# Two-layer decoder trunk: first layer up to its norm rewritten, with no large GpSimd operations in that stretch

## Chip, cores, metric

One core of a Trainium2 chip. The metric is the device time of one execution in microseconds (us). The engines are called as the profile calls them: PE (TensorE), DVE (VectorE), ACT (ScalarE), POOL (GpSimd), SP (SyncE, which here only issues DMAs). Each has its own instruction stream, and they meet at semaphores.

## What is computed

Two layers on 512 tokens of width 1024; the feed-forward width is 2816. All is float32. Cut to what matters here:

```python
mod = silu(c) @ ada_w + ada_b            # six vectors of 1024 per layer: t1, s1, g1, t2, s2, g2
h = x * (1 + s1) + t1
a, u, v = split(h @ w_in)                # 4 groups of 128 | 512 | 512
pooled = (cs - prev) / cnt - a           # trailing windows 2, 4, 8, 16 over the tokens
pool = (pooled @ pool_w) * pool_scale
v = layernorm(gelu(v)) * sgu_ln_g + sgu_ln_b
z = tril(sgu_w) @ v + sgu_b              # per head, in chunks of 128 tokens
f = concat(pool, gelu(u) * z) @ w_out
x = layernorm(ALPHA * x + g1 * f)        # n1
...                                      # channel mixing with t2, s2, g2, then n2
```

## The kernel before

Every product is done as three float32r matmuls: a weight is split into a rounded upper part `whi` and the rest `wlo`, an activation into `hh` and `hl`, and `mm3` adds up whi·hh, whi·hl and wlo·hh. A weight of 128x1024 (512 KB) goes through `load` (L65, issued by SP), a cast on ACT to `whi` (L132) and a subtraction to `wlo` (L135), which `refill` puts on DVE or, with `G`, on POOL. Seven raw buffers (`N_RAW`) hold weights and adaLN matrices alike; a load waits until the operation that read its buffer before is done.

The adaLN vectors are sums on DVE (`ada_sum`, L182): a 128x1024 piece of `ada_w` times silu(c), accumulated to one column. Sixteen of them (`raw_first`) give t1 and s1 of the first layer, 24 more (`raw_ada`) the three vectors that its first norm needs. `pump` puts them between other work; each step also issues loads `ADA_AHEAD` steps ahead.

The scheduler is manual: each engine takes its instructions as the code writes them, and SP its DMAs. The stages of the first layer:

1. The first stage, a loop over the eight k-tiles of h: two sums (L182), A0 and B0 (L462, L465), `hh` on DVE (L466), the same in float32 on ACT (L467), `hl` (L468, on DVE for k below 2, else on POOL), and the products of this k-tile for the four tiles of a and the four chunks of v, 192 matmuls of 512 columns in all.
2. Token mixing: copies of a (L532), trailing sums (L540, L541) and pooled (L550 to L553), the norm of v (gelu L574, statistics L577, `rstd_of` L272 to L275 with the power on POOL, two DVE operations L280 and L283), four tiles of u, `pool_mix` (L560 to L565), `z_mms` (L603) and `z_mix` (L586 to L597).
3. The projection with `w_out`, the second half of it in `project_and_norm`: per chunk the residual (L291, L292), statistics (L377), `rstd_of`, the application (L383), the transposition on PE (`turn`, L298) and `modulate` (L310 to L313), which gives the `hh` and `hl` that the next products read. The lower parts of the next weights are made in it, on POOL (`refill(..., G, lows)`).
4. `after_norm`, the next stage's first four tiles; `next_residuals` then runs eight operations on POOL (L318, L319) that multiply the norm's rows g and b (loaded by L325, scaled on ACT, L327) into xr. `project_and_norm` and `next_residuals` run three times: at the norm n1 of layer 0, at n2 of layer 0 and at n1 of layer 1.

Of the kernel before, what the change touches and what calls it, by code (L numbers as in the profile page):

```python
# [8 lines left out]
F32 = mybir.dt.float32  # L9
# [18 lines left out]
N_UNITS, N_RAW, N_SPLIT = 29, 7, 6  # L28
AHEAD, ADA_AHEAD = 2, 3
PRE_FILL, FILL = 6, (0, 2, 2, 2, 2, 3)  # L30
# [8 lines left out]
def trunk(ctx: ExitStack, tc: tile.TileContext, a: dict, out: bass.AP):  # L39
# [5 lines left out]
    wraw = ctx.enter_context(tc.tile_pool(name="wraw", bufs=N_RAW))  # L45
    wsplit = ctx.enter_context(tc.tile_pool(name="wsplit", bufs=N_SPLIT))
# [4 lines left out]
    # each engine takes its instructions in the order they are written here  # L51
# [24 lines left out]
    A.activation(c_th, c_in, AF.Tanh, scale=0.5)  # L76
    V.scalar_tensor_tensor(c_th, c_th, 1.0, c_in, op0=ALU.add, op1=ALU.mult)
    c2 = const.tile([P, D], F32, name="c2")
    for hf in range(2):
        ps = bank(f"c2_{hf}")  # L80
        for j in range(4):
            k = 4 * hf + j
            T.matmul(
                ps[:, j * P : (j + 1) * P], c_th[:, k : k + 1].to_broadcast([P, P]), ident, start=True, stop=True
            )
        A.copy(c2[:, halves(hf)], ps)
    ones = const.tile([P, P], F32, name="ones")
    V.memset(ones, 1.0)
# [4 lines left out]
    rcnt = const.tile([P, 16], F32, name="rcnt")  # L93
    modc = [const.tile([P, 48], F32, name=f"modc{l}") for l in range(L)]

    # ---- the weights in the order of their use: float32 in, two float32r parts out
# [56 lines left out]
    def refill(n=1, eng=None, defer=None, in_units=False):  # L153
        """Prepares the next n weights, as far as there is room for them."""
        for _ in range(n):
            if count["split"] < len(order) and (in_units or count["live"] < N_SPLIT):
                wsplit_next(in_units, eng, defer)
                while count["load"] < min(len(order), count["split"] + count["ahead"]):
                    wload()

    def get():
        assert ready
        return ready.pop(0)
# [4 lines left out]
    def mm3(ps, w, x, start, stop):  # L168
        """ps += (wh + wl).T @ (xh + xl)"""
# [4 lines left out]
    # ---- adaLN: columns of silu(c) @ ada_w, 128 at a step, that fill in between other work  # L174
# [54 lines left out]
    def pump(n=1, upto=None):  # L229
        """n steps of the sums, as far as these are for the vectors upto."""  # L230
# [14 lines left out]
    def weave(gens, side=()):  # L245
        """The steps of gens in turn, those of side in between."""
# [6 lines left out]
    def affine_cols(l, sub, g, b):  # L253
        """Columns A, B with h = n * A + B, from the last norm's g and b and the modulation."""
# [14 lines left out]
    # ---- post-norm: xr holds the sum; leaves n, h, and the next residual  # L269
# [8 lines left out]
    def affine_norm(t, mv, rs, g, b, pieces=1, after=None):  # L278
        """t = (t - mean) * rstd * g + b"""
# [7 lines left out]
    def residual(ps, c, hf, gate, eng=None, f=slice(0, HALF)):  # L287
        """Columns f of half hf."""
# [5 lines left out]
    def turn(c, tag):  # L294
        """n of one chunk, transposed."""
# [5 lines left out]
    def modulate(c, ps, tag, AB):  # L301
        """h of one chunk from its transposed n, in two halves."""
# [27 lines left out]
    def pair_mms(ps, c, w, act, i, n, f=slice(0, HALF)):  # L330
        """A pair of k-tiles i, i + 1 of n, for columns f of one chunk."""
# [8 lines left out]
    def project(act, hf, name, after):  # L340
        """All chunks at once against streamed weights; after(i) follows each pair."""
# [11 lines left out]
    def project_and_norm(act, ps0, gate, tag, AB):  # L353
        """The second half chunk by chunk, each chunk's norm under the next one's products.
        ps0 holds the first half. Leaves the last chunk to be turned."""
# [5 lines left out]
        for c in range(NCH):  # L361
# [6 lines left out]
            if c == NCH - 1:  # L368
                refill(4 - len(ready), G, lows)
# [16 lines left out]
            if c + 1 < NCH:  # L386
                residual(ps0[c + 1], c + 1, 0, gate, G)

    def project_and_end(act, ps0, gate, grow, brow):
        """The same at the end, where the norm goes out; the last chunk's columns in two parts."""  # L390
# [7 lines left out]
        def first_half(c):  # L398
            sts[c] = small.tile([P, 4, 6], F32, tag="st4", name=f"end{c}")
            residual(ps0[c], c, 0, gate, G)  # L400
# [47 lines left out]
    # ---- start: modulation of the first layer and h from x, one k-tile after the other  # L448
# [3 lines left out]
    def first_load(k):  # L452
        x = unit(f"xT{k}")
        raw = [load(a["ada_w"][0, v, k], f"first{v}_{k}") for v in (1, 0)]
# [3 lines left out]
    def first_h(k, x, raw):  # L458
# [21 lines left out]
    tiles, v_w = [], []  # L480
    for k in range(KD):
# [23 lines left out]
    wload(3)  # L505
    refill(1, G)
    count["ahead"] = AHEAD
    done = [ps for ps, w in tiles]

    for l in range(L):  # L510
        col = cols[l]

        # ======== token mixing
# [19 lines left out]
        sums = []  # L533

        def window_sums(g, eng):
            s = at[g]
            for i in range(g + 1):
                d = 1 << i
                n = unit(f"ws{g}_{i}")
                eng.tensor_tensor(n[:, d:], s[:, d:], s[:, : S - d], op=ALU.add)  # L540
                eng.tensor_copy(n[:, :d], s[:, :d])  # L541
                s = n
            sums.append(s)

        pooled = []

        def pool_group(g):
            w, s = WINDOWS[g], sums[g]
            t = unit(f"pooled{g}")
            V.scalar_tensor_tensor(t, s, 1.0 / w, at[g], op0=ALU.mult, op1=ALU.subtract)  # L550
            e = small.tile([P, 16], F32, tag="edge", name=f"edge{g}")
            V.tensor_tensor(e[:, : w - 1], s[:, : w - 1], rcnt[:, : w - 1], op=ALU.mult)
            V.tensor_tensor(t[:, : w - 1], e[:, : w - 1], at[g][:, : w - 1], op=ALU.subtract)  # L553
            pooled.append(t)

        mix = [None] * 8

        def pool_mix(g):
            ps = bank(f"pm{g}")
            T.matmul(ps, poolw[:, g * P : (g + 1) * P], pooled[g], start=True, stop=True)  # L560
            sc = col[:, C_PS + g : C_PS + g + 1]
# [22 lines left out]
        def z_mix(h):  # L584
            z = unit(f"z{h}")
            V.tensor_tensor(  # L586
                z.rearrange("p (c t) -> p c t", c=NCH),
                z_ps[h].rearrange("p (c t) -> p c t", c=NCH),
                sb[:, h * P : (h + 1) * P].unsqueeze(1).to_broadcast([P, NCH, P]),
                op=ALU.add,  # L590
            )
            yield
# [18 lines left out]
        lo_eng = None if l else G  # L611
        if l:
            v_ps = [bank(f"v{l}_{c}") for c in range(NCH)]
            for k in range(KD):
# [3 lines left out]
                if k % 2:  # L618
                    free(w)
                    window_sums(k // 2, V)  # L620
                    pool_group(k // 2)
                    refill(1)
        else:
            pump(PRE_FILL, fill)
            refill(1, G)
        w3 = wst.rearrange("p (h t) -> p h t", h=4)
        G.affine_select(
            out=w3, in_=w3, pattern=[[0, 4], [1, P]], compare_op=ALU.is_ge, fill=0.0, base=0, channel_multiplier=-1
        )
        side = [] if l else [refill]  # L630
        weave([v_norm(c, v_ps[c]) for c in range(NCH)], side + [lambda: pump(1, fill)] * FILL[0])
        if l == 0:
            window_sums(0, V)
            window_sums(1, V)
            pool_group(0)
            pool_group(1)
        u = []
        for i in range(4):
            w, ps = get(), bank(f"u{i}")
            feature_mms(ps, w)  # L640
            free(w)
            ada_flush()
            refill(2 if l == 0 and i < 2 else 1, lo_eng)
            u.append(unit(f"u{i}"))
            A.activation(u[i], ps, AF.Gelu_apprx_tanh)
            if l == 0:
                nc.sync.dma_start(xr[i], a["x"][i * P : (i + 1) * P, :])
            work = []
            if i == 0 and l == 0:
# [150 lines left out]
```

## Time and profile before

| | |
|---|---|
| three runs | 1043.29, 1040.75, 1042.89 us; median 1042.89 us |
| profiled execution, its span | 1041.6 us |
| PE busy | 990.9 us, 95% of the span |
| DVE, ACT, POOL busy | 695.7, 352.8, 214.0 us |
| first stage | 0 to 67.6 us of the span |
| token mixing of layer 0 and its projection, until the adaLN vectors are there | 67.6 to 149.5 us |
| norm n1 of layer 0, first tiles of channel mixing | 149.5 to 205 us |

The profiled execution is known by its span alone. Times in rows count from the span's start. A row of the timeline gives start, duration, engine, line, operation, output and inputs, and in brackets how long the engine was idle before it and what ended that. The clock is that granted to PE, as a share of 2.4 GHz.

### The profile page before, as it was taken

To read this page: it belongs to the slowest core of one execution; us is meant where nothing else is said; L and a number is where in the kernel's file an instruction comes from. 1 tells how busy PE (TensorE), PEld (TensorE's weight loads), DVE (VectorE), ACT (ScalarE), POOL (GpSimd) and SP (SyncE) were. 2 spreads that over 40 slices of the span, in tenths; PEclk is the share of its full clock that TensorE was granted. 3 is DMA by queue.
4 is the path that set the end of the run, shared out by engine and by line. 5 is a ranking of instruction groups with operands and counts; after the bars stand their busy time and mean duration, and the time that the engine had idled before them with its cause. 6 is when DMAs were issued, how large, how long until landed. Compare 5 with 4: busy or idle time off the path is not lost.

```text
span 1041.6 us, 11987 instructions
## 1 busy us (share of the span) xinstructions
PE 990.9 (95%) x4654; PEld 826.8 (79%) x4654; DVE 695.7 (67%) x896; ACT 352.8 (34%) x495; POOL 214.0 (21%) x136
## 2 busy tenths in 40 slices
PE   5996889999999999999999999999999999999996
PEld 4785568888888888888888878888888888888886
DVE  6989998788673456757579973878744245444446
ACT  3242316443432123334254331644343212333210
POOL 4647245800000000000039300680000000000022
PEclk7998899999999999999999999999999999999999
DMA  9873772276574336547603422227433332334002
GB/s 334 306 276 110 287 279 76 90 259 211 194 228 135 102 101 200 183 147 257 203 21 114 160 81 81 83 94 250 141 101 101 101 101 81 101 101 142 21 1 81
DMA packets 44695, 154.57 MB, mean 148 GB/s; under 512 B 5216, under 2 KB 5472, under 8 KB 44640
## 3 DMA queue, kind: packets, MB, share of 16 engines
q1 hardware_dynamic: 44640, 153.82, 43.6%
q8 instruction: 36, 0.59, 0.2%
q14 instruction: 19, 0.16, 0.0%
HBM read 151.71 MB, written 2.10 MB: 148 GB/s over the span
## 4 chain that ended last, share of the span: by engine, by line
PE 82%; DVE 10%; POOL 3%; DMA 2%; issue 2%; ACT 1%; SPq 0%; DVEq 0%; POOLq 0%; ACTq 0%
PE up L171 15%; PE up L172 15%; PE up L170 15%; PE down L336 6%; PE down L338 6%; PE down L337 6%; PE n_pj L336 2%; PE n_pj L338 2%; PE n_pj L337 2%; DVE raw_ada L182 2%; POOL wlo L135 1%; DMA b<-in_ln_b_dram 1%; PE out L338 1%; PE v L475 1%; PE v L476 1%
## 5 line engine op out<-in xcount | busy, mean ns | idle before, releaser
L171 PE MATMUL up<-hl,whi 128*128 128x512 f32 (+1 forms) x768 | 285.6, 372 | 4.8 <-DVE hl L313 4.8
L172 PE MATMUL up<-hh,wlo 128*128 128x512 f32 (+1 forms) x768 | 285.4, 372 | 1.0 <-POOL wlo L135 1.0
L170 PE MATMUL up<-hh,whi 128*128 128x512 f32 (+1 forms) x768 | 285.5, 372 | 0.0
L135 DVE TENSOR_TENSOR wlo<-raw_w_up,whi 128x1024 fp32r<-128x1024 f32 x81 | 111.7, 1381 | 135.6 <-ACT whi L132 135.6
L171 PEld LDWEIGHTS up<-hl,whi 128*128 128x128 f32 x768 | 144.6, 188 | 30.5 <-DVE hl L313 5.6
L172 PEld LDWEIGHTS up<-hh,wlo 128*128 128x128 f32 x768 | 144.6, 188 | 26.4 <-POOL wlo L135 1.4
L170 PEld LDWEIGHTS up<-hh,whi 128*128 128x128 f32 x768 | 144.6, 188 | 24.9
L135 DVE TENSOR_TENSOR wlo<-raw_w_down,whi 128x1024 fp32r<-128x1024 f32 x44 | 53.9, 1225 | 114.0 <-ACT whi L132 114.0
L132 ACT CAST whi<-raw_w_up 128x1024 fp32r<-128x1024 f32 x88 | 91.0, 1045 | 69.1 <-PE down L338 52.6
L182 DVE SCALAR_TENSOR_TENSOR raw_ada<-raw_ada,c 128x1024 f32<-128x1024 f32 x80 | 106.4, 1341 | 4.1 <-DMA raw_ada<-in_ada_w_dram 4.1
L336 PE MATMUL down<-whi,gh 128*128 128x512 f32 x272 | 105.8, 389 | 0.0
L337 PE MATMUL down<-wlo,gh 128*128 128x512 f32 x272 | 105.8, 389 | 0.0
L338 PE MATMUL down<-whi,gl 128*128 128x512 f32 x272 | 105.8, 389 | 0.0
L274 POOL TENSOR_SCALAR rs_n<-mv_n 128x1 f32<-128x1 f32 x12 | 5.8, 485 | 397.5 <-DVE mv_n L272 397.5
L292 POOL TENSOR_TENSOR xr<-res,xr 128x512 f32<-128x512 f32 x13 | 16.6, 1289 | 321.8 <-DVE res L291 319.6
L694 ACT ACTIVATE y<-y 128x512 f32<-128x512 f32 x44 | 27.9, 634 | 148.8 <-DVE y L691 148.8
L132 ACT CAST whi<-raw_w_down 128x1024 fp32r<-128x1024 f32 x44 | 46.0, 1047 | 74.8 <-PE down L338 74.8
L684 ACT ACTIVATE y<-up,cols 128x512 f32<-128x512 f32 x44 | 34.3, 779 | 80.0 <-PE up L172 80.0
L338 PEld LDWEIGHTS down<-whi,gl 128*128 128x128 f32 x272 | 51.1, 188 | 10.6
L336 PEld LDWEIGHTS down<-whi,gh 128*128 128x128 f32 x272 | 51.1, 188 | 10.6
L337 PEld LDWEIGHTS down<-wlo,gh 128*128 128x128 f32 x272 | 51.1, 188 | 10.6
L310 ACT ACTIVATE ht_n<-tr_n,B,A 128x128 f32<-128x128 f32 x96 | 36.1, 455 | 57.2 <-PE tr_n L298 41.2
(155 smaller groups left out, 1620.7 us busy)
## 6 DMA issues: line engine op xcount, KB each, us to landing
raw_w_up<-in_w_up_dram SPq DMA_DIRECT2D x88, 512.0 KB, 3.3
raw_ada<-in_ada_w_dram SPq DMA_DIRECT2D x80, 512.0 KB, 4.2
raw_w_down<-in_w_down_dram SPq DMA_DIRECT2D x44, 512.0 KB, 3.3
raw_w_in<-in_w_in_dram SPq DMA_DIRECT2D x24, 512.0 KB, 4.3
raw_first<-in_ada_w_dram SPq DMA_DIRECT2D x16, 512.0 KB, 5.3
raw_w_out<-in_w_out_dram SPq DMA_DIRECT2D x16, 512.0 KB, 4.1
xT<-in_xT_dram SPq DMA_DIRECT2D x8, 256.0 KB, 5.4
xr<-in_x_dram SPq DMA_DIRECT2D x4, 512.0 KB, 6.5
```

Source lines behind the costliest of these rows:

```text
L132: A.copy(hi, src)
L135: (eng or V).tensor_tensor(lo, src, hi.bitcast(F32), op=ALU.subtract)
L170: T.matmul(ps, w[0], x[0], start=start, stop=False)
L171: T.matmul(ps, w[0], x[1], start=False, stop=False)
L172: T.matmul(ps, w[1], x[0], start=False, stop=stop)
L182: V.scalar_tensor_tensor(raw, raw, 0.5, c2, op0=ALU.mult, op1=ALU.mult, accum_out=modc[l][:, o : o + 1])
L310: A.activation(tmp[:, w], ps[hf][:, w], AF.Identity, bias=cb[:, k : k + 1], scale=ca[:, k : k + 1])
L336: T.matmul(ps[:, f], ah[:, cs], wh, start=i + j == 0, stop=False)
L337: T.matmul(ps[:, f], ah[:, cs], wl, start=False, stop=False)
L338: T.matmul(ps[:, f], al[:, cs], wh, start=False, stop=i + j == n - 1)
L684: A.activation(y, pg, AF.Identity, bias=col[:, C_CB + j : C_CB + j + 1], scale=col[:, cw + 2 : cw + 3])
L694: A.activation(y, y, AF.Gelu_apprx_tanh)
```

## The change

- Seven raw buffers become four for weights (`N_RAW`) and three for adaLN pieces (`N_ADA`); `ADA_AHEAD` goes from 3 to 2.
- In the first stage `hh` is made on ACT; all `hl` and all `wlo` are made on DVE. The broadcast of silu(c) is 16 float32r matmuls in place of eight float32 ones.
- The norm of v takes its sum from the gelu and its sum of squares from another pass on ACT; one DVE operation (new L597) applies it. That norm's gain and bias are moved behind the chunk products: `z_mix` multiplies by a column `sgc` and adds `zb`, made once per layer by one 512-column float32 matmul (`rw`) and four DVE operations. Two row loads per layer (`sg`, `sbt`) go, four small column loads come.
- The trailing sums are all on DVE, without a separate operation for the first tokens' result; 1/w goes into `psc`, four tiny operations.
- The mixing stage of layer 0 is written out by hand; all 24 `raw_ada` sums come behind the u tiles.
- In `project_and_norm` the three deferred `wlo` and the first-half residuals of the next chunk go from POOL to DVE. `next_residuals` stays on POOL.

```diff
-N_UNITS, N_RAW, N_SPLIT = 29, 7, 6
-AHEAD, ADA_AHEAD = 2, 3
-PRE_FILL, FILL = 6, (0, 2, 2, 2, 2, 3)
+N_UNITS, N_RAW, N_ADA, N_SPLIT = 29, 4, 3, 6
+AHEAD, ADA_AHEAD = 2, 2
+P2_FILL, OUT_FILL = 3, (3, 3, 4, 4)
...
-                refill(4 - len(ready), G, lows)
+                refill(4 - len(ready), None, lows)
...
-                residual(ps0[c + 1], c + 1, 0, gate, G)
+                residual(ps0[c + 1], c + 1, 0, gate)
...
-        V.tensor_scalar(hh[:, k, :], x, A0[:, o], B0[:, o], op0=ALU.mult, op1=ALU.add)
+        A.activation(hh[:, k, :], x, AF.Identity, bias=B0[:, o], scale=A0[:, o])
         A.activation(x, x, AF.Identity, bias=B0[:, o], scale=A0[:, o])
-        (V if k < 2 else G).tensor_tensor(hl[:, k, :], x, hh[:, k, :].bitcast(F32), op=ALU.subtract)
+        for f in late:
+            f()
+        late.clear()
+        V.tensor_tensor(hl[:, k, :], x, hh[:, k, :].bitcast(F32), op=ALU.subtract)
...
+            nm, ss = [small.tile([P, 1], F32, tag=n, name=f"{n}{l}_{c}") for n in ("vnm", "vss")]
+            A.activation(t, ps, AF.Gelu_apprx_tanh, accum_out=nm)
+            A.activation(nm, nm, AF.Copy, scale=-1.0 / HALF)
+            A.activation(ps, t, AF.Square, bias=nm, accum_out=ss)
             yield
-            V.bn_stats(st[:, 0, :], t)
-            mv, rs = rstd_of(st, f"v{c}")
+            G.tensor_scalar(ss, ss, 1.0 / HALF, EPS, op0=ALU.mult, op1=ALU.add)
+            G.tensor_tensor(ss, ss, neg_half, op=ALU.pow)
             yield
-            affine_norm(t, mv, rs, sg, sbt)
+            V.tensor_scalar(t, t, nm, ss, op0=ALU.add, op1=ALU.mult)
...
+            ps = u_tile(3)
+            step(pms)
+            pms = step([pool_mix(2), pool_mix(3)])
+            u_gelu(3, ps)
+            refill(1)
+            step(pms)
+            for c in range(NCH):
+                nc.sync.dma_start(xr[c], a["x"][c * P : (c + 1) * P, :])
+            z_mms()
+            pump(P2_FILL, fill)
+            zs = step([z_mix(0), z_mix(1)])
+            refill(1)
+            step(zs)
+            zs = step([z_mix(2), z_mix(3)])
+            refill(1)
+            step(zs)
         def after_out(i):
-            refill(1, lo_eng)
-            pump(FILL[5], fill)
+            refill(1)
+            pump(OUT_FILL[i // 2], fill)
```

DVE in the first stage, k-tile 1, before and after the change (`raw_first` is a sum, `hl` the k-tile's lower part):

```order
L182 SCALAR_TENSOR_TENSOR raw_first_1_167,modc_111<-raw_first_1_167,c_91 128x1024
L182 SCALAR_TENSOR_TENSOR raw_first_1_169,modc_111<-raw_first_1_169,c_91 128x1024
L462 SCALAR_TENSOR_TENSOR A_0_119<-modc_111,cols_80 128x1
L465 TENSOR_TENSOR B_0_120<-modc_111,cols_80 128x1
L466 TENSOR_SCALAR hh<-xT_166,A_0_119,B_0_120 128x512
L468 TENSOR_TENSOR hl<-xT_166,hh 128x512
```

```order
L194 SCALAR_TENSOR_TENSOR raw_first_1_186,modc_130<-raw_first_1_186,c_102 128x1024
L194 SCALAR_TENSOR_TENSOR raw_first_1_188,modc_130<-raw_first_1_188,c_102 128x1024
L474 SCALAR_TENSOR_TENSOR A_0_138<-modc_130,cols_83 128x1
L477 TENSOR_TENSOR B_0_139<-modc_130,cols_83 128x1
L483 TENSOR_TENSOR hl<-xT_185,hh 128x512
L147 TENSOR_TENSOR wlo_201<-raw_w_in_191,whi_200 128x1024
```

`hh` has left DVE's row and `wlo` has come into it, behind `hl`.

SP at the first `raw_ada` loads, before and after the change (`xr` is x for the residual):

```order
L65 DMA raw_ada_503<-in_ada_w_dram 128x1024
...
L65 DMA raw_ada_524<-in_ada_w_dram 128x1024
L65 DMA raw_w_in_531<-in_w_in_dram 128x1024
L65 DMA raw_w_out_546<-in_w_out_dram 128x1024
L65 DMA raw_w_out_632<-in_w_out_dram 128x1024
```

```order
L66 DMA raw_w_out_767<-in_w_out_dram 128x1024
L713 DMA xr_134<-in_x_dram 128x1024
L713 DMA xr_135<-in_x_dram 128x1024
L713 DMA xr_136<-in_x_dram 128x1024
L713 DMA xr_137<-in_x_dram 128x1024
L66 DMA raw_ada_795<-in_ada_w_dram 128x1024
L66 DMA raw_ada_797<-in_ada_w_dram 128x1024
L66 DMA raw_ada_799<-in_ada_w_dram 128x1024
```

Nine `raw_ada` loads stood ahead of the last `w_in`; now the first one stands behind four `w_out` loads and all of x.

POOL at the norm n2 of layer 0, last chunk, before and after the change (`rs` is the reciprocal deviation):

```order
L274 TENSOR_SCALAR rs_n_0_3_4050<-mv_n_0_3_4048 128x1
L275 TENSOR_TENSOR rs_n_0_3_4050<-rs_n_0_3_4050,neg_half 128x1
L135 TENSOR_TENSOR wlo_4025<-raw_w_in_3788,whi_4024 128x1024
L135 TENSOR_TENSOR wlo_4028<-raw_w_in_3796,whi_4027 128x1024
L318 TENSOR_TENSOR xr_115<-xr_115,g_3617 128x1024
L319 TENSOR_TENSOR xr_115<-xr_115,b_3618 128x1024
```

```order
L286 TENSOR_SCALAR rs_n_0_3_4059<-mv_n_0_3_4057 128x1
L287 TENSOR_TENSOR rs_n_0_3_4059<-rs_n_0_3_4059,neg_half 128x1
L330 TENSOR_TENSOR xr_134<-xr_134,g_3626 128x1024
L331 TENSOR_TENSOR xr_134<-xr_134,b_3627 128x1024
L330 TENSOR_TENSOR xr_135<-xr_135,g_3626 128x1024
```

The two `wlo` are gone from POOL (they stand on DVE, ahead of the last application), and `next_residuals` follows the power directly.

## Rows read from the trace of the kernel before

**Rows 1.** The page: busy time of each engine.
```profile
PE 990.9 (95%) x4654; PEld 826.8 (79%) x4654; DVE 695.7 (67%) x896; ACT 352.8 (34%) x495; POOL 214.0 (21%) x136
```
**Rows 2.** Stretches: length, busy PE, PEld, DVE, ACT, POOL, granted clock, DMA share, GB/s.
```profile
14.00:28.00 14.00, 10.65 (x28) 7.80 (x29) 13.04 (x16) 2.85 (x4) 7.62 (x3) 0.64 0.90 333
38.50:67.64 29.14, 29.14 (x129) 24.12 (x130) 25.79 (x36) 9.42 (x12) 15.23 (x8) 1.00 0.86 301
67.64:149.50 81.86, 68.51 (x281) 53.41 (x280) 79.56 (x109) 24.91 (x34) 43.46 (x28) 0.90 0.64 231
205.00:515.00 310.00, 310.00 (x1370) 256.66 (x1369) 199.22 (x276) 104.17 (x129) 0.07 (x1) 1.00 0.57 186
```
**Rows 3.** Timeline of PE, with what ended its idle time, to 156 us.
```profile
38.48 0.50 PE L171 MATMUL a<-hl,whi 128*128 128x512 f32 x1 [1.76 <-POOL hl L468]
67.64 0.39 PE L170 MATMUL u<-hh,whi 128*128 128x512 f32 x1
106.26 1.02 PE L560 MATMUL pm<-pooled,poolw 128*128 128x512 f32 x2
155.61 1.75 PE L298 MATMUL tr_n<-ident,xr 128*128 128x128 f32 x7 [4.91 <-DVE xr L383]
```
**Rows 4.** Groups of DVE, then of POOL, 7.4 to 149.5 us: busy, mean ns | idle before.
```profile
L182 DVE SCALAR_TENSOR_TENSOR raw_ada<-raw_ada,c 128x1024 f32<-128x1024 f32 x24 | 38.2, 1630 | 4.1 <-DMA raw_ada<-in_ada_w_dram 4.1
L135 POOL TENSOR_TENSOR wlo<-raw_w_in,whi 128x1024 fp32r<-128x1024 f32 x11 | 30.9, 2819 | 20.6 <-ACT whi L132 20.6
```
**Rows 5.** Timeline of DVE, 7 to 148 us: the same operations, quick and slow.
```profile
7.46 1.23 DVE L182 SCALAR_TENSOR_TENSOR raw_first<-raw_first,c 128x1024 f32<-128x1024 f32 x1 [4.15 <-ACT c L86]
16.93 3.38 DVE L182 SCALAR_TENSOR_TENSOR raw_first<-raw_first,c 128x1024 f32<-128x1024 f32 x1
71.00 1.23 DVE L135 TENSOR_TENSOR wlo<-raw_w_in,whi 128x1024 fp32r<-128x1024 f32 x1 [0.37 <-ACT whi L132]
113.19 1.29 DVE L593 TENSOR_TENSOR z<-z,u 128x512 f32<-128x512 f32 x2
149.49 0.68 DVE L291 TENSOR_TENSOR res<-out,gate 128x512 f32<-128x512 f32 x1
```
**Rows 6.** Groups of ACT, 7.4 to 149.5 us.
```profile
L132 ACT CAST whi<-raw_w_in 128x1024 fp32r<-128x1024 f32 x12 | 12.4, 1043 | 11.6 <-DMA raw_w_in<-in_w_in_dram 11.6
L467 ACT ACTIVATE xT<-xT,B,A 128x512 f32<-128x512 f32 x8 | 6.5, 816 | 30.9 <-DVE hh L466 30.9
```
**Rows 7.** The loads of raw_ada: from 100 to 160 us; the page, over the whole span.
```profile
DMA to landing us min/median/max: 3.2/4.9/7.8
raw_ada<-in_ada_w_dram SPq DMA_DIRECT2D x80, 512.0 KB, 4.2
```
**Rows 8.** Timelines at the norm n1 of layer 0, last chunk: ACT, POOL, DVE, PE.
```profile
182.35 1.06 ACT L327 ACTIVATE b<-b 128x1024 f32<-128x1024 f32 x1 [0.22 <-DMA b<-in_ln_b_dram]
185.49 4.92 DVE L313 TENSOR_TENSOR hl<-ht_n,hh 128x512 fp32r<-128x512 f32 x2 [3.51 <-ACT hh L312]
190.47 0.39 PE L171 MATMUL up<-hl,whi 128*128 128x256 f32 x1 [1.11 <-DVE hl L313]
```
**Rows 9.** Timelines at n2 of layer 0, last chunk (154.74: n1, first chunk).
```profile
547.16 5.15 POOL L135 TENSOR_TENSOR wlo<-raw_w_in,whi 128x1024 fp32r<-128x1024 f32 x2
552.27 2.86 POOL L318 TENSOR_TENSOR xr<-xr,g 128x1024 f32<-128x1024 f32 x1
154.74 0.81 DVE L383 TENSOR_SCALAR xr<-xr,mv_n,rs_n 128x1024 f32<-128x1024 f32 x1 [1.00 <-POOL rs_n L275]
545.70 0.21 DVE L272 BATCH_NORM_AGGREGATE mv_n<-stn 128x2 f32<-128x12 f32 x1
547.24 2.85 DVE L383 TENSOR_SCALAR xr<-xr,mv_n,rs_n 128x1024 f32<-128x1024 f32 x1 [0.77 <-POOL rs_n L275]
550.14 1.09 PE L298 MATMUL tr_n<-ident,xr 128*128 128x128 f32 x8 [1.86 <-DVE xr L383]
558.42 16.79 DVE L135 TENSOR_TENSOR wlo<-raw_w_in,whi 128x1024 fp32r<-128x1024 f32 x5
```
**Rows 10.** Timeline of PE at the norm n1 of layer 1, end of the last wait.
```profile
684.57 0.39 PE L171 MATMUL up<-hl,whi 128*128 128x256 f32 x1 [1.10 <-DVE hl L313]
```

More of the change, by code (lines that the diff above doesn't have):

```diff
@@ L82, in trunk @@
             k = 4 * hf + j
-            T.matmul(
-                ps[:, j * P : (j + 1) * P], c_th[:, k : k + 1].to_broadcast([P, P]), ident, start=True, stop=True
-            )
+            for i, part in enumerate(c_hl):
+                T.matmul(
+                    ps[:, j * P : (j + 1) * P],
+                    part[:, k : k + 1].to_broadcast([P, P]),
+                    ident_r,
+                    start=i == 0,
+                    stop=i == 1,
+                )
         A.copy(c2[:, halves(hf)], ps)
-    ones = const.tile([P, P], F32, name="ones")
-    V.memset(ones, 1.0)
     ones_r = const.tile([P, P], F32R, name="ones_r")
@@ L399, in first_half @@
             sts[c] = small.tile([P, 4, 6], F32, tag="st4", name=f"end{c}")
-            residual(ps0[c], c, 0, gate, G)
+            residual(ps0[c], c, 0, gate)
         def first_stats(c):
@@ L527, in trunk @@
         nc.sync.dma_start(sb, a["sgu_b"][l : l + 1, :].partition_broadcast(P))
+        if l == 0:
+            nc.sync.dma_start(rcnt, a["rcnt"])
+            nc.sync.dma_start(cols[1], a["cols"][1])
+            with nc.allow_non_contiguous_dma(reason="columns of the gating norm"):
+                for t, n in ((sgc, "sgu_ln_g"), (sbc, "sgu_ln_b")):
+                    for i in range(L):
+                        nc.sync.dma_start(t[:, i, :], a[n][i].rearrange("(h d) -> d h", h=4))
         at = []
@@ L539, in window_sums @@
                 n = unit(f"ws{g}_{i}")
-                eng.tensor_tensor(n[:, d:], s[:, d:], s[:, : S - d], op=ALU.add)
-                eng.tensor_copy(n[:, :d], s[:, :d])
+                V.tensor_tensor(n[:, d:], s[:, d:], s[:, : S - d], op=ALU.add)
+                V.tensor_copy(n[:, :d], s[:, :d])
                 s = n
[L543 to L556, printed above, removed]
+            V.scalar_tensor_tensor(s[:, : w - 1], s[:, : w - 1], float(w), rcnt[:, : w - 1], op0=ALU.mult, op1=ALU.mult)
+            V.scalar_tensor_tensor(s, at[g], -float(w), s, op0=ALU.mult, op1=ALU.add)
+            pooled.append(s)
+        psc = small.tile([P, 4], F32, tag="psc", name=f"psc{l}")
+        for g in range(4):
+            V.tensor_scalar(psc[:, g : g + 1], col[:, C_PS + g : C_PS + g + 1], 1.0 / WINDOWS[g], None, op0=ALU.mult)
         def pool_mix(g):
@@ L609, in z_mms, with u_tile, u_gelu, step @@
                     )
-        lo_eng = None if l else G
+        u = []
+        def u_tile(i):
+            w, ps = get(), bank(f"u{i}")
+            feature_mms(ps, w)
+            free(w)
+            ada_flush()
+            u.append(unit(f"u{i}"))
+            return ps
+        def u_gelu(i, ps):
+            A.activation(u[i], ps, AF.Gelu_apprx_tanh)
+        def step(gens):
+            return [g for g in gens if next(g, 0) is None]
+        w3 = wst.rearrange("p (h t) -> p h t", h=4)
+        G.affine_select(
+            out=w3, in_=w3, pattern=[[0, 4], [1, P]], compare_op=ALU.is_ge, fill=0.0, base=0, channel_multiplier=-1
+        )
         if l:
@@ L635, in trunk @@
             pool_group(0)
+            norms = step([v_norm(c, v_ps[c]) for c in range(NCH)])
+            ps = u_tile(0)
             pool_group(1)
[L637 to L649, printed above, removed]
-                window_sums(2, V)
-                window_sums(3, G)
-                pool_group(2)
-            if i == 1 and l == 0:
-                pool_group(3)
-            if i == 2:
-                z_mms()
-                work = [z_mix(0), z_mix(1), pool_mix(0), pool_mix(1)]
-            if i == 3:
-                work = [pool_mix(2), pool_mix(3), z_mix(2), z_mix(3)]
-            weave(work, [lambda: pump(1, fill)] * FILL[i + 1])
+            norms = step(norms)
@@ new lines, in trunk @@
+            zbias = z_bias()
+            next(zbias)
+            u_gelu(0, ps)
+            refill(1)
+            ps = u_tile(1)
+            step(norms)
+            u_gelu(1, ps)
+            pool_group(2)
+            refill(1)
+            ps = u_tile(2)
+            pms = step([pool_mix(0), pool_mix(1)])
+            u_gelu(2, ps)
+            next(zbias, 0)
+            pool_group(3)
+            refill(1)
+            ps = u_tile(3)
+            step(pms)
+            pms = step([pool_mix(2), pool_mix(3)])
```

97 lines of the change are left out of this document (57 added, 40 removed).

## Prediction

> **What bounds the kernel now.** I began with the page's busy times: PE works 95% of the span [rows 1], so only its waits and its half-clock stretches can give anything, about 50 us in all. Then the stretches. From 205 to 515 us PE is busy for the whole 310 us [rows 2]; no change on DVE or POOL gains there. From 38.5 to 67.64 us PE is full too. The slack lies between: from 67.64 to 149.5 us DVE is busy 79.56 of 81.86 us and PE 68.51 [rows 2]. So DVE sets the end of that stretch, and the stretch ends when the last adaLN sum is done and the first residual starts, at 149.49 [rows 5]. PE had nothing to do for 4.91 us then [rows 3].
>
> Why is DVE that full? Its groups show it: 24 sums with a mean of 1630 ns [rows 4], while a quiet sum takes 1.23 us and a disturbed one 3.38 [rows 5]. The disturbed ones lie beside POOL's `wlo`, eleven of which take 2819 ns each [rows 4]. On DVE alone a `wlo` is 1.23 [rows 5]. The change takes POOL's big operations out of this stretch. The rule of the Trainium skill for it (SBUF — State Buffer, "Who interferes with whom": a DVE operation with two SBUF inputs and a GpSimd operation that reads SBUF lock each other out for a whole instruction, and issue order decides who waits) agrees on these rows; it is weighed below, where it speaks against the change.
>
> The forecast is of the span, 1041.6 us; the median of the runs is 1042.9, so 1.3 are added at the end. A change under 0.3%, 3.1 us, counts as no change.
>
> **First stage.** PE's last 129 matmuls of this stage run without a gap from 38.48, where they waited for POOL's `hl` [rows 3], to 67.64: 29.2 us [rows 2], 0.227 each. What counts is when the `hl` of k-tile 3 is there. By hand on DVE, without POOL: two sums 2.30 (1.15 from start to start), A0 and B0 0.31, a wait for two ACT passes of 0.82 each [rows 6] and their start 1.72, `hl` 0.61, a wait for the cast 0.43, and 1.15 for each `wlo`: 6.5 us for a k-tile with one `wlo`, 7.7 with two. The first sum waited for the broadcast of silu(c) until 7.46 [rows 5]; that is cheaper on PE now, and I take 6.4, about where the sum's data land. k-tiles 0 to 2 cost 7.7 + 6.5 + 7.7 = 21.9, then 4.95 to the `hl` of k-tile 3: 33.3, and PE starts at 33.7. It ends at 63.0 in place of 67.64, **4.6 us earlier**. If PE is still at half clock when it does k-tile 2, as it was for much of 14 to 28 us (granted 0.64 [rows 2]), it ends at 65.3: 2.3 earlier.
>
> **Token mixing.** DVE's work shrinks (no slow sums, one operation for v's norm in place of bn_stats and two), but 15 `wlo` come to it at 1.15, 17 us. PE first sets the pace: four u tiles at 24 matmuls x 0.227 = 5.44, the `rw` product 0.5 and four `pm` at 0.51 [rows 3]: 63.0 + 21.8 + 2.5 = 87.4. After that come a pass and a cast on ACT (0.82 and 1.04 [rows 6], with waits 2.2), a `wlo` and two `ml` on DVE, 2.4: 92.0. Then 22.5 us of DVE: twelve z and `ml` operations at 0.64 [rows 5], 7.7; four `wlo`, 4.6; six sums, 6.9; waits for ACT's casts at 1.04 [rows 6], 3.3. That is 114.5 with six sums done.
>
> The remaining 18 go through three buffers. A buffer is loaded again only when its sum is done: 3.2 us to landing at the least [rows 7], 1.15 for the sum, 0.15 to issue, so 4.5 per three sums, 27.0 for 18. The rest of DVE's list in that time (the gate's diagonals 2.7, two `wlo` 2.3) is hidden for a small part; I add 4.5. Last sum done at 146.0, the five small operations behind it 0.7: **146.7 in place of 149.49, −2.8.** With u at 65.3 it is −0.6. DVE is no longer slowed, but it now waits for DMA: of the 4.6 us of the first stage nearly half is lost here, since the loads stand behind x and `w_out`.
>
> **Norm n1 of layer 0.** The same chain starts 2.8 earlier. The row loads of g and b no longer wait for POOL's `wlo`; b's scaling, which holds up ACT before the last `modulate` [rows 8], comes about 3 us sooner. DVE gets three `wlo` more, 3.5 us, and the last chunk's application stands behind them; while DVE does them, PE has products of the other chunks' tokens to do, and without that cover they would take the gain away. POOL's next residuals still lie beside the last two `hl` (4.92 for two [rows 8]). Channel mixing's second token half starts at 187.4 in place of 190.47: **−3.0**, after which PE is full and keeps it.
>
> **Norm n2 of layer 0.** Here the change makes a wait. Before, POOL did two `wlo` from 547.16 to 552.27 and then began the next residuals [rows 9]. Now these follow the power at once, and DVE has the `wlo` ahead of the last application. Before, that application took 2.85 beside POOL, where a quiet one takes 0.81 [rows 9]. DVE's list after the statistics is now `wlo`, `wlo`, `hl`, application. The statistics end at 545.9 [rows 9]; the two `wlo` take 2.3 in quiet and reach across the point where POOL starts, then `hl` and the application each lose a turn to POOL: PE turns the chunk at 551.2 to 552.7 in place of 550.14. I take 551.3, **+1.2**, the end nearer to the row. By the Trainium skill's rule named above, in which issue order decides, either side can hold the port: with POOL ahead each time this term is +2.5, with DVE ahead −1.7. No row here has DVE ahead.
>
> **Norm n1 of layer 1.** The same change of order, but here POOL has to wait for g to be loaded and scaled, and by the same durations the last `hl` ends at 684.3, where PE started at 684.57 [rows 10]: **−0.3**; the best is −2.4. **Layer 1** has one more float32 matmul on PE's full path, `rw`: 0.51 from the `pm` rows [rows 3], **+0.5**; in layer 0 it is inside the slack counted above. v's norm on ACT in layer 1 is hidden under the u tiles (ACT has 0.82 per pass [rows 6], PE 5.44 per tile). The small loads and `psc` cost nothing beside these: they are under 0.2 each and stand ahead of a wait; without that cover 1 us. The tail is not touched but for two residuals, which lie under products.
>
> Sum: −3.0 + 1.2 − 0.3 + 0.5 = −1.6. 1041.6 − 1.6 = 1040.0 in the span, with 1.3 more **1041.3 us**.
>
> **The other ways it could go.**
>
> *Faster, 1036.3.* At the two later norms DVE gets its turn before POOL. Then the application is 0.81 rather than 2.85, n2 gives −1.7 and n1 of layer 1 −2.4: −3.0 − 1.7 − 2.4 + 0.5 = −6.6. For it: DVE waits for the same semaphore as POOL, and the two residuals that left POOL free its queue. Against it: at 547.24 DVE lost this race by 0.08 us [rows 9].
>
> *Slower, 1047.3.* The three buffers. The sum took the shortest landing, 3.2. The median in this stretch was 4.9, and 4.2 over the whole span [rows 7]; part of that was queueing behind other loads, which the smaller ring makes less. If it stays at 4.2 beside `w_out` and `w_up`, each of the six rounds costs 1.0 more, the last sum comes at 152.0 and the adaLN vectors at 152.7: +3.2 in place of −2.8, and the sum is −1.6 + 6.0 = +4.4. The point from which it decides is a landing of 3.7, where the gain of 2.8 is gone. Nothing else is on that path: DVE would show waits for `raw_ada`, which were 4.1 us in all before [rows 4].
>
> *No change.* DVE gains by quiet sums, 24 x 0.4 = 9.6 (1.63 against 1.23 [rows 4, 5]), and pays more for `wlo`, 17; and the half clock keeps u at 65.3: −0.6 − 0.2 at n1, +1.2 −0.3 + 0.5 = +0.6, 1043.5. Another page bears on this (the Trainium skill, Perfetto Trace Analysis, "Optimizing Scalar/DVE Operations": with a saturated DVE, moving work off it can pay, but GpSimd and DVE share a port, so between these two it may not). By it, work that goes the other way, on to a DVE busy 97% of the stretch, pays only as far as the rows' quiet times hold.
>
> **How the numbers follow.** Forecast 0.40, faster 0.28, slower 0.20, no change 0.12. Of the forecast's own range (−4 to +2, from the two ends of the first stage and of n2) 0.05 lies below −3.1. So faster 0.33, same 0.47, slower 0.20. The range, 1036.0 to 1047.5, just takes in the times of the faster and the slower case; about a third of each, 0.16 together, lies beyond.
>
> **What would show it.** First stage: the first u matmul at 63 to 65, no DVE sum over 1.3 us before 150. Token mixing: waits of DVE for `raw_ada` of 5 us or more, the first residual near 146.7; later than 150 and the slower case holds. n2: POOL's first next residual right behind the power near 547, PE's turn of the last chunk later than 1 us against the chunk's other work; if it is sooner, the faster case. If POOL still shows long operations before 150, the change doesn't do what it says. A PE wait anywhere from 205 to 515 would make the whole account wrong.

## The result: 12 us slower, beyond the slower of the forecast's cases

The changed kernel takes 1055.15 us in the median (1054.78 to 1057.14) against 1042.88 before: ratio 1.0129, 95% interval 1.0112 to 1.0146 (the two medians alone give 1.0118). Its profiled span is 1053.7 us, 12.1 more than before. The median lies above the range given, 1036.0 to 1047.5, and above the slower case, 1047.3.

The page of the changed kernel, as [rows 1], shows what the change was written to do: POOL's busy time falls from 214 to 101 us, DVE's from 696 to 666. PE has the same work to do.

```profile
PE 990.8 (94%) x4658; PEld 828.0 (79%) x4658; DVE 666.1 (63%) x931; ACT 367.5 (35%) x535; POOL 101.4 (10%) x80
```

The stretches of the changed kernel, in the columns of [rows 2]: PE's full part of the first stage, from u's first product to the first residual of n1, and full channel mixing.

```profile
33.50:62.48 28.98, 28.98 (x128) 23.68 (x127) 18.58 (x37) 13.62 (x17) 1.66 (x1) 1.00 0.85 290
62.48:155.33 92.85, 66.73 (x287) 52.23 (x285) 68.31 (x125) 28.61 (x49) 3.89 (x8) 0.88 0.62 217
...
210.00:520.00 310.00, 310.00 (x1370) 256.62 (x1369) 201.54 (x278) 103.59 (x129) 0.29 (x1) 1.00 0.53 184
```

Before, token mixing was 81.86 us long with DVE busy for 79.56; now it is 92.85 long with DVE busy for 68.31. DVE has less to do and finishes later: it waits. The groups of DVE, 7.4 to 156 us, answer to [rows 4]:

```profile
L194 DVE SCALAR_TENSOR_TENSOR raw_ada<-raw_ada,c 128x1024 f32<-128x1024 f32 x24 | 28.8, 1222 | 11.2 <-DMA raw_ada<-in_ada_w_dram 10.9
L194 DVE SCALAR_TENSOR_TENSOR raw_first<-raw_first,c 128x1024 f32<-128x1024 f32 x16 | 18.9, 1220 | 4.0 <-ACT c L99 4.0
L147 DVE TENSOR_TENSOR wlo<-raw_w_in,whi 128x1024 fp32r<-128x1024 f32 x12 | 14.6, 1225 | 9.2 <-ACT whi L144 9.2
```

Every sum is quiet, 1.22 us where [rows 4] had 1.63. But the waits for `raw_ada` have grown to 10.9 us. The loads of `raw_ada` from 90 to 157 us (as in [rows 7]; the first line is DVE's idle time and how often, the last the time to landing, from a load's issue until its data are there):

```profile
  DMA raw_ada<-in_ada_w_dram: 10.9, 8
...
DMA to landing us min/median/max: 3.2/4.6/6.9
```

The milestones show where the 12.1 us arose (to turn a chunk is to transpose it on PE). On PE and DVE of the changed kernel, as in [rows 3, 5, 8, 9]:

```profile
62.48 0.39 PE L182 MATMUL u<-hh,whi 128*128 128x512 f32 x1
...
155.33 0.68 DVE L303 TENSOR_TENSOR res<-out,gate 128x512 f32<-128x512 f32 x1
...
161.46 0.88 PE L310 MATMUL tr_n<-ident,xr 128*128 128x128 f32 x3 [14.68 <-DVE xr L395]
...
196.60 0.58 PE L183 MATMUL up<-hl,whi 128*128 128x256 f32 x1 [0.79 <-DVE hl L325]
...
561.38 0.90 PE L310 MATMUL tr_n<-ident,xr 128*128 128x128 f32 x3 [4.70 <-DVE xr L395]
...
688.23 0.98 PE L310 MATMUL tr_n<-ident,xr 128*128 128x128 f32 x7 [2.46 <-DVE xr L395]
```

| milestone | before | changed | difference |
|---|---|---|---|
| u's first product | 67.64 | 62.48 | −5.2 |
| adaLN vectors there, first residual of n1 | 149.49 | 155.33 | +5.8 |
| PE turns the first chunk at n2 of layer 0 | 526.1 | 534.5 | +8.4 |
| PE turns the last chunk at n2 of layer 0 | 550.14 | 561.38 | +11.2 |
| PE turns the first chunk at n1 of layer 1 | 651.9 | 666.3 | +14.4 |
| PE turns the last chunk at n1 of layer 1 | 673.70 | 688.23 | +14.5 |
| end of the span | 1041.6 | 1053.7 | +12.1 |

So: +5.8 from the adaLN sums; +2.6 up to n2; +2.8 in n2's own wait (4.70 in place of 1.86); +3.2 behind it; −2.3 at n1 of layer 1, where the two waits for `hl` are gone. Most of the +2.6 and of the +3.2 is half clock, 1.2 in place of 2.4 GHz, which stands behind two of the waits in the changed kernel and not before:

```profile
195.00:202.00 7.00, 6.21 (x31) 5.92 (x30) 7.00 (x3) 1.31 (x2) 6.92 (x3) 0.51 0.17 44
560.00:567.00 7.00, 5.62 (x27) 5.62 (x28) 6.36 (x4) 4.41 (x11) 6.92 (x4) 0.52 0.00 0
```

In each of the two PE falls 2.3 us further behind the kernel before: from 6.1 at the second wait for `hl` in n1 (196.60 against 190.47) to 8.4 at n2's first chunk, and from 11.2 at n2's last chunk to 13.5 at the first product of u in layer 1 (603.91 against 590.39). The rest of the +3.2 is `rw`, which stands behind the first of u's four tiles. The second product behind it comes 14.4 later than before, so `rw` costs 0.9. In the changed kernel, then before:

```profile
609.36 1.02 PE L604 MATMUL rw<-wst,ones 128*128 128x512 f32 x2
610.45 0.40 PE L183 MATMUL u<-hl,whi 128*128 128x512 f32 x1
...
596.06 0.39 PE L171 MATMUL u<-hl,whi 128*128 128x512 f32 x1
```

### The profile page after: what moved, and what is told of

Its sections match the earlier page's. It is cut to its first block, busy times and chain, and to the rows that moved or that the text cites. A ratio compares the mean times of both kernels' runs of the same rounds, so it can differ in the third digit from the quotient of the medians.

```text
span 1053.7 us, 11969 instructions
## 1 busy us (share of the span) xinstructions
PE 990.8 (94%) x4658; PEld 828.0 (79%) x4658; DVE 666.1 (63%) x931; ACT 367.5 (35%) x535; POOL 101.4 (10%) x80
## 4 chain that ended last, share of the span: by engine, by line
PE 81%; DVE 11%; DMA 4%; ACT 2%; issue 1%; POOL 1%; SPq 0%; DVEq 0%; POOLq 0%; ACTq 0%
PE up L183 15%; PE up L184 15%; PE up L182 15%; PE down L348 6%; PE down L350 6%; PE down L349 6%; DMA raw_ada<-in_ada_w_dram 2%; DVE wlo L147 2%; DVE raw_ada L194 1%; PE u L184 1%; PE u L183 1%; PE u L182 1%; DVE res L303 1%; DVE stn L389 1%; DVE xr L304 1%
## 5 line engine op out<-in xcount | busy, mean ns | idle before, releaser
L147 DVE TENSOR_TENSOR wlo<-raw_w_up,whi 128x1024 fp32r<-128x1024 f32 x88 | 120.0, 1369 | 137.7 <-ACT whi L144 137.7
L194 DVE SCALAR_TENSOR_TENSOR raw_ada<-raw_ada,c 128x1024 f32<-128x1024 f32 x80 | 97.0, 1219 | 11.2 <-DMA raw_ada<-in_ada_w_dram 10.9
L147 DVE TENSOR_TENSOR wlo<-raw_w_in,whi 128x1024 fp32r<-128x1024 f32 x24 | 35.5, 1498 | 14.3 <-ACT whi L144 14.0
```

The source lines that it names most:

```text
L147: (eng or V).tensor_tensor(lo, src, hi.bitcast(F32), op=ALU.subtract)
L194: V.scalar_tensor_tensor(raw, raw, 0.5, c2, op0=ALU.mult, op1=ALU.mult, accum_out=modc[l][:, o : o + 1])
```

## Experiments

The theory after the result: the three-deep ring for adaLN pieces (buffers loaded in turn, each again when its sum is done) sets the end of the sums; a lock-out between DVE and POOL at n2 adds its wait. Rivals: the sums merely start too late; DVE's new `wlo` at n2 are the cause, not POOL. Eight kernels were run. Ratios are against the kernel before, which ran on the same chip each time, with 95% intervals.

| kernel | median us | ratio | last of the 24 sums ends at | first residual of n1 |
|---|---|---|---|---|
| the change | 1055.15 | 1.0129 [1.0112, 1.0146] | 154.6 | 155.33 |
| e1, six sums early | 1046.93 | 1.0037 [1.0024, 1.0049] | 151.2 | 151.84 |
| e8, four buffers | 1045.64 | 1.0032 [1.0017, 1.0048] | 149.4 | 150.11 |
| e2, five buffers | 1041.92 | 0.9981 [0.9968, 0.9994] | 144.2 | 144.91 |
| e3, deferred `wlo` on POOL | 1055.27 | 1.0112 [1.0094, 1.0130] | 156.0 | 156.72 |
| e4, next residuals held back | 1046.98 | 1.0031 [1.0019, 1.0044] | 156.6 | 157.28 |
| e7, before with the change's buffers | 1048.98 | 1.0066 [1.0042, 1.0090] | 155.0 | 155.73 |
| e6, before, next residuals held back | 1038.36 | 0.9963 [0.9949, 0.9977] | 149.0 | 149.72 |
| e5, e1 + e2 + e4 | 1029.13 | 0.9868 [0.9848, 0.9889] | 138.3 | 138.95 |

The two times on the right are from one profile each. The change, e3 and e4 have the same ring and the same order up to there, and end the last sum at 154.6, 156.0 and 156.6: a difference of 2 us in these columns shows nothing.

### e2 and e8: the depth of the ring

```diff
-N_UNITS, N_RAW, N_ADA, N_SPLIT = 29, 4, 3, 6
-AHEAD, ADA_AHEAD = 2, 2
+N_UNITS, N_RAW, N_ADA, N_SPLIT = 25, 4, 5, 6
+AHEAD, ADA_AHEAD = 2, 4
```

> The changed kernel with five buffers for adaLN pieces in place of three and loads four steps ahead (N_UNITS 25 in place of 29 makes the room). The order of the sums stays. If the three-deep ring is what stretches the sums, their pace from 116 us on falls from 2.1 us to about 1.4, DVE's waits for raw_ada (about 11 us between 116 and 155) go below 4, and the first residual comes at 145 to 148: 7 to 10 us faster than the changed kernel. If the late start and the transfers themselves (about 23 loads of 1.28 us behind 113 us) set the end, the gain is 1 to 4 us.

With five buffers the last sum ends 10.4 us earlier. The loads of `raw_ada` in e2, from 58 to 160 us:

```profile
  DMA raw_ada<-in_ada_w_dram: 0.4, 1
...
DMA to landing us min/median/max: 3.3/5.5/11.0
```

A load takes longer there than in the change (5.5 against 4.7 over the same stretch), and DVE hardly waits. So transfers did not set the end, as the rival had it: the number of loads under way did. (Buffers and look-ahead go up together here, and `N_UNITS` goes down; in e7 below `N_UNITS` stays.) The kernel gained 13 us, more than the sums: n2's wait fell to 2.2 and the half clock behind n1 and n2 of layer 0 did not occur. It stands behind the wait of 2.45 at n1 of layer 1 instead, where the changed kernel, with 2.46, keeps full clock. In e2, then in the change:

```profile
670.00:676.00 6.00, 4.34 (x25) 4.34 (x26) 2.35 (x5) 4.31 (x8) 5.15 (x3) 0.72 0.73 235
...
688.00:695.00 7.00, 6.78 (x57) 6.78 (x58) 6.36 (x4) 6.47 (x13) 6.92 (x3) 1.00 0.42 138
```

e8 has 27, 4, 4, 6 and three steps ahead.

> The changed kernel with four buffers for adaLN pieces and loads three steps ahead (N_UNITS 27). If the depth of the ring sets the pace of the last 18 sums, one round of n sums takes a landing (median 4.6 us with three buffers) and a sum (1.15): 1.9 us a sum with three, 1.45 with four. Last sum then about 147 us (154.6 with three, 144.2 with five), DVE's waits for raw_ada between 1 and 4 us (10.9 with three, 0.4 with five), total about 1044 to 1048. If five helped for another reason (fewer units, another order on SP), four lies nowhere between.

Four buffers lie between: last sums at 154.6, 149.4 and 144.2 with three, four and five, about 5 us for each buffer, and DVE's waits are 10.9, 5.0 and 0.4.

```profile
  DMA raw_ada<-in_ada_w_dram: 5.0, 6
...
DMA to landing us min/median/max: 3.1/5.3/10.6
```

The expectation was 2 us too good for four: the landing took 5.3, against 4.7 in the change over the same stretch. What lengthens it is not shown: with three buffers it is 5.5 in e1 and 5.1 in e4. The ring is shown, and its price is that of the landing as it is in the kernel at hand. Here too the total falls by more than the sums: n2's wait is 2.19, as in e2.

### e7: the ring alone, in the kernel before

```diff
-N_UNITS, N_RAW, N_SPLIT = 29, 7, 6
-AHEAD, ADA_AHEAD = 2, 3
+N_UNITS, N_RAW, N_ADA, N_SPLIT = 29, 4, 3, 6
+AHEAD, ADA_AHEAD = 2, 2
...
-                ada_raw.append(load(a["ada_w"][ada[i]], f"ada{i}"))
+                ada_raw.append(load(a["ada_w"][ada[i]], f"ada{i}", araw))
...
-        raw = [load(a["ada_w"][0, v, k], f"first{v}_{k}") for v in (1, 0)]
+        raw = [load(a["ada_w"][0, v, k], f"first{v}_{k}", araw) for v in (1, 0)]
```

> The kernel before with the change's buffers alone: four for weights and three for adaLN pieces instead of seven for both, loads two steps ahead instead of three. The sums stay where they were, six of them before the u tiles. If a ring of three is short by itself, DVE waits for raw_ada by more than the 4.1 us of before and the first residual comes later than 149.5, by 2 to 6 us: 1045 to 1049. If it is short only because the change puts all 24 sums in one run behind the u tiles, no difference within 1.5 us: before, POOL's lock-outs make each sum last 1.6 us, which gives a load time to land.

The buffers alone, with none of the rest of the change, put the first residual at 155.73, 6.2 us later than before, and cost 0.66%. DVE's waits for `raw_ada`, 58 to 157 us:

```profile
  DMA raw_ada<-in_ada_w_dram: 12.3, 6
...
DMA to landing us min/median/max: 3.2/4.3/8.9
```

The four buffers for weights, which come with the ring, are not the cause. SP issues its loads in order, and in the same stretch it waits 75.7 us in all for a sum to free a buffer and 0.6 for a weight's `wlo`:

```profile
SPq L66 <- DVE raw_ada L183: 75.7, 19, 27.6
...
SPq L66 <- DVE wlo L136: 0.6, 1, 0.6
```

With e2 this closes the question from both sides: with a ring of three the kernel before loses what the change lost up to the first residual, and with a ring of five the change is 0.2% faster than before.

### e1: an earlier start, three buffers kept

```diff
     wload(2)
+    ada_load(N_ADA)
...
             pool_group(1)
+            pump(3, fill)
...
             step(pms)
+            pump(3, fill)
             pms = step([pool_mix(2), pool_mix(3)])
```

> The changed kernel with six of the 24 raw_ada sums pulled forward: the first three loads are issued at the end of the first stage, three sums follow the second trailing-sum group, three more the lower parts of the first two pm products. Buffers stay at three. If the late start of the sums is what delays the adaLN vectors (all 24 stand behind the u tiles, their loads behind four w_out and all of x), then 18 sums are left after 93 us in place of 24, at the 2.1 us a sum that the changed kernel shows, six sums are worth about 11 us: the first residual of n1 near 144 us in place of 155.3, the whole 9 to 12 us faster than the changed kernel, 1043 to 1046. If the three buffers alone set the end, whatever the start (each round of three waits for a landing), the later sums stretch and less than 5 us is gained: first residual later than 150.

This went as the ring had it, not the late start: six sums fewer behind the u tiles, and the first residual only 3.5 us earlier (151.84, later than 150). DVE's waits for `raw_ada` from 90 us on rose from 10.9 to 14.6 us for 18 sums. The total still fell by 8 us, since n2's wait was 2.2 and PE's half clock behind n1 did not occur (behind n2 it did, granted 0.66 from 553 to 558 us). The expected total was nearly met for another reason than the one given.

### e3 and e4: who makes PE wait in the norms

```diff
-                refill(4 - len(ready), None, lows)
+                refill(4 - len(ready), G, lows)
```

> The changed kernel with one word put back: the three deferred lower parts in project_and_norm on POOL again. If their move to DVE is what lengthens PE's wait at n2 of layer 0 (4.7 us in the changed kernel, 1.9 before), by putting POOL's next residuals directly behind the power, then that wait goes back to about 2, the half-clock stretch behind it disappears, and n1 of layer 1 loses some of what it gained: 2 to 5 us faster than the changed kernel, about 1051. If DVE's own work is the cause and not POOL's place, no difference within 1 us.

A miss: no change in the total, as the other branch had it, but not for its reason. n2's wait did go down, to 1.35, but PE waits 3.78 us at each of the two other norms, where the changed kernel has 0.72 and 2.46, with half clock behind both (0.50 from 186 to 191 us, 0.61 from 687 to 691). At n1 of layer 0 and of layer 1:

```profile
186.82 0.58 PE L184 MATMUL up<-hh,wlo 128*128 128x256 f32 x1 [3.78 <-POOL wlo L147]
...
687.15 1.12 PE L310 MATMUL tr_n<-ident,xr 128*128 128x128 f32 x4 [3.78 <-DVE xr L395]
```

The move of the deferred `wlo` to DVE was thus worth about as much at the two n1 as it cost at n2.

```diff
     def next_residuals(grow, brow):
+        tiny = small.tile([P, 1], F32, tag="vss", name="tiny")
+        G.tensor_copy(tiny, hl[:, KD - 1, S - 1 : S].bitcast(F32))
```

> The changed kernel with one tiny POOL operation ahead of the next residuals that reads the last column of hl, so that the eight large POOL operations begin only when the last chunk's hl is written. If the lock-out between DVE and POOL makes PE wait in the three norms, DVE's application there is 0.8 us and each hl 0.7: the wait at n2 of layer 0 falls below 2 us, the waits for hl at n1 of layer 0 (1.8 and 0.8) fall below 0.5 each, half-clock stretches behind both vanish: 6 to 9 us faster than the changed kernel, 1046 to 1049. If POOL is then late for something (the residuals that come next, or the lower parts that run beside it), the gain is given back and the time stays within 2 us or rises.

8 us faster, with the adaLN sums as late as ever. The chunk at n2 of layer 0, in the changed kernel (POOL, then DVE):

```profile
553.31 0.22 POOL L286 TENSOR_SCALAR rs_n<-mv_n 128x1 f32<-128x1 f32 x1 [6.77 <-DVE mv_n L284]
553.61 1.48 POOL L287 TENSOR_TENSOR rs_n<-rs_n,neg_half 128x1 f32<-128x1 f32 x1
555.06 2.96 POOL L330 TENSOR_TENSOR xr<-xr,g 128x1024 f32<-128x1024 f32 x1
...
553.44 2.36 DVE L147 TENSOR_TENSOR wlo<-raw_w_in,whi 128x1024 fp32r<-128x1024 f32 x2 [0.22 <-issue]
555.72 2.86 DVE L325 TENSOR_TENSOR hl<-ht_n,hh 128x512 fp32r<-128x512 f32 x1
558.50 2.82 DVE L395 TENSOR_SCALAR xr<-xr,mv_n,rs_n 128x1024 f32<-128x1024 f32 x1
```

The same chunk's DVE in e4:

```profile
550.91 2.36 DVE L147 TENSOR_TENSOR wlo<-raw_w_in,whi 128x1024 fp32r<-128x1024 f32 x2 [0.22 <-issue]
553.18 0.69 DVE L325 TENSOR_TENSOR hl<-ht_n,hh 128x512 fp32r<-128x512 f32 x1
553.79 0.81 DVE L397 TENSOR_SCALAR xr<-xr,mv_n,rs_n 128x1024 f32<-128x1024 f32 x1
```

and in e2, where POOL and DVE do what they do in the change (POOL, then DVE):

```profile
541.54 1.08 POOL L286 TENSOR_SCALAR rs_n<-mv_n 128x1 f32<-128x1 f32 x1 [6.77 <-DVE mv_n L284]
542.71 1.40 POOL L287 TENSOR_TENSOR rs_n<-rs_n,neg_half 128x1 f32<-128x1 f32 x1
544.08 2.42 POOL L330 TENSOR_TENSOR xr<-xr,g 128x1024 f32<-128x1024 f32 x1
...
541.37 2.31 DVE L147 TENSOR_TENSOR wlo<-raw_w_in,whi 128x1024 fp32r<-128x1024 f32 x2
543.60 0.68 DVE L325 TENSOR_TENSOR hl<-ht_n,hh 128x512 fp32r<-128x512 f32 x1
544.20 2.84 DVE L395 TENSOR_SCALAR xr<-xr,mv_n,rs_n 128x1024 f32<-128x1024 f32 x1
```

In the change POOL's tiny operation got in 0.13 us ahead of DVE's `wlo` and took 0.22; in e2 it came 0.17 behind and took 1.08. That puts POOL's first big operation 0.66 ahead of DVE's `hl` in the change and 0.48 behind it in e2. In the change `hl` and the application each lose their turn to POOL (2.86, 2.82), in e2 the application alone, and PE waits 4.70 or 2.2. e1 and e8 show e2's order, with 2.19 each. In e4 neither loses it; there PE's waits for `hl` at n1 of layer 0 are 0.34 each, and no half clock stands behind n1 or n2 of layer 0. What holds DVE back by 0.22 in the change isn't settled.

The rival, DVE's own `wlo`, is told apart by e4 too. Both still stand ahead of the application there, and PE waits 0.50 at n2: the rest of the 4.70 came with POOL. At n1 of layer 1 it is the other way. PE waits 2.44 in e4 as well, with POOL's large operations held back and the application at 0.81: there it is the two `wlo` on DVE that PE waits for.

### e6: the same hold in the kernel before

The edit of e4, with the tile's tag "rs".

> The kernel before with the next residuals on POOL held back until the last hl is written. If the lock-out is what PE waits for in the norms, the waits at 186.2 and 189.4 (1.45 and 1.11 us) and at 680.7 and 683.5 (1.12 and 1.10) go; the waits for the last application (1.28 at 178, 1.86 at 548, 1.28 at 672) stay, since POOL's own lower parts, not the next residuals, lie beside it there. 3 to 5 us faster than before, 1038 to 1040. If POOL's eight operations then delay the lower parts behind them on DVE, the gain is given back: within 1 us of before.

As expected in the total and nearly so in its parts: 0.37% faster, three of the four waits for `hl` gone and the first down from 1.45 to 0.34, and the waits for the application still there (1.30, 1.85 and 1.30 us). No engine waits for what POOL's eight operations write. Behind n2's wait PE falls to half clock here (granted 0.72 from 547 to 553 us), which it did not before behind a wait of 1.86.

### e5: the version that beats both

The edits of e1, e2 and e4 together.

> The changed kernel with the three edits together: five buffers and loads four steps ahead, six sums pulled forward, next residuals held back until the last hl. If the three causes are separate, the first residual comes at 134 to 138 us (144.9 with five buffers, six sums at 1.2 to 1.7 us less), and the wait at n2 of layer 0 falls from 2.2 to 0.5, those for hl at n1 go: 1027 to 1033. If DVE or DMA is full already with five buffers (DVE is busy 53.2 of 60 us from 90 to 150 there), the early sums gain less than 4 us: 1035 to 1038.

1029.13 us, 1.3% under the kernel before and, by the two ratios, 2.6% under the change (0.9868 over 1.0129). The first residual stands at 138.95, a microsecond later than the range expected. DVE was busy 68.0 of the 77 us up to there, and waits 2.3 for `raw_ada`, so there is little left to win from the loads. PE's wait at n2 is gone; the one at n1 of layer 1 stays at 2.45, with half clock behind it (0.64 from 660 to 664 us). Up to the first residual:

```profile
62.00:139.00 77.00, 70.16 (x289) 54.11 (x287) 68.00 (x125) 28.98 (x49) 6.12 (x8) 0.93 0.70 253
```

## Why the prediction was wrong

**What bounds.** Right: only what lies outside channel mixing moved, PE is full in 210 to 520 us as before, and the end of the stretch to n1's first residual was set by DVE's chain of sums. No sum lasts longer than 1.23 us.

**First stage.** Right in mechanism; the size came out by two misses that cancel: u starts at 62.48 (63.0 to 65.3 were given). The first sum did not start earlier (7.46 again, where 6.4 was taken: the broadcast's products end at 6.80 as they did at 6.81 before, and the copy of c on ACT follows). But k-tiles 0 to 2 took 1.3 less than reckoned, so the `hl` of k-tile 3 was there at 33.0 (33.3 reckoned), and PE showed no half clock there.

**Token mixing: the failed step.** "A buffer is loaded again only when its sum is done: 3.2 us to landing at the least [rows 7], 1.15 for the sum, 0.15 to issue, so 4.5 per three sums, 27.0 for 18." The mechanism was right; the term was sized with the shortest landing of [rows 7], and its median was there too, 4.9. In the changed kernel the median was 4.6. The 18 last sums ran from 116.41 to 154.64, 2.12 each, where 31.5 us in all, 1.75 each, had been reckoned: 6.7 us more, with a start 1.9 later. That is 8.6 on the last sum, and what the forecast had as −2.8 came out as +5.8. The loads issued from 114 to 132 us landed after 4.1 to 6.9 us. The reason given for a shorter landing, less queueing with the smaller ring, took 0.3 off the median (4.9 before and 4.6 now, 90 to 157 us), not 1.7. (By the Trainium skill, SBUF — State Buffer, "The DMA setup-cost knee", a transfer takes about 2 us and its bytes over 436 GB/s, an estimate of 3.2 us for 512 KB: the trace agrees for the shortest landing, 3.2, and no row here shows that as the usual one.)

A landing longer than 3.2 was the slower rival. It gave 152.0 for the last sum at a landing of 4.2, and was itself too low. It was worth 0.20 to the forecast; the row itself, whose median was past the 3.7 from which that rival decides, asked for more than half.

Of the 1.9 by which the start was late, 1.4 was there when PE's products ended, at 88.8 where 87.4 was reckoned. In the `pm` row of [rows 3] the 1.02 us with x2 is one float32 product, which stands as two records (as `rw` does above), and was read as two.

**n1 of layer 0.** The lead of 3 us was not there to pass on. A wait that the prediction took from before (1.11 for `hl`) stayed (1.80 and 0.79), and PE fell to half clock behind it, 2.3 us of the +2.6. The term ended with "after which PE is full and keeps it": half clock behind a wait was put at nothing, here and at n2, 4.6 us in all. e2 has waits of 1.77 and 1.10 there and no half clock behind them. So these waits alone don't decide, and what does is open.

**n2 of layer 0.** Right in place and cause, too small: +1.2 was taken, +2.5 with POOL ahead each time; the wait grew by 2.8, and half clock behind it cost 2.3 more. The rule that was weighed there (the Trainium skill, SBUF — State Buffer, "Who interferes with whom": whoever issues first holds the shared port for the whole instruction) is what these rows show: beside POOL `hl` took 2.86 and the application 2.82, where they take 0.69 and 0.81 in e4. The end taken was the nearer to the row; the rows of the other runs show an order that turns on some tenths.

**n1 of layer 1.** −0.3 was given, the best being −2.4; it was −2.3. **`rw`** was reckoned at +0.5 from the `pm` row, by the reading told above, and cost 0.9.

**The faster rival** had DVE win both turns. In the changed kernel it did so at n1 of layer 1 (2.3 gained) and lost at n2. **No change** is excluded: the interval of the ratio begins at 1.0112.

## What to carry to other kernels

A ring of n buffers gives n results per landing and use; size it with the median landing of a stretch that is as busy with loads, not with the shortest, and expect it to differ from kernel to kernel (3.9 to 5.3 us with three buffers here, 90 to 157 us). When work is moved to a place where its results are the last thing waited for, the ring decides when the stage ends. If two engines hold each other up, ask which of them can wait: one tiny operation that makes the engine off the path wait for the path's last result was worth 8 us here, and about 4 in the kernel before.

## What was not expected of the hardware

- Beside DVE's `wlo` the tiny POOL power took 1.40 to 1.48 us, where it takes 0.57 in the kernel before at the same place, with no `wlo` on DVE beside it: operations of 128x1 are held up as well, and POOL can be the one that waits.
- An order of 0.13 to 0.17 us between two operations, one 128x1, went with waits of 2.2 or 4.7 us on PE (2.2 in e1, e2 and e8, 4.7 in the change). No run changes that order alone.
- A wait's cost on PE was up to nearly twice its length, where half clock stood behind it (0.51 from 195 to 202 us, behind 1.80 and 0.79). With waits as long (1.77 and 1.10 in e2) it didn't occur, and behind 2.45 at n1 of layer 1 it did in e2, e5 and e8 and not in the change. What decides is open.
